# The fourth pair of HGRN2's queries by 512-column products, in a one-core decoder block

## The chip, the cores and the metric

One core of one Trainium2 chip runs the whole kernel as one launch. The metric is the device time of that launch in microseconds (us). TensorE is PE in the profile, its weight loads PEld, VectorE is DVE, ScalarE is ACT, GpSimd is POOL; SP issues most transfers.

## The reference

A decoder block on 256 tokens of width 1024. One input projection feeds two mixers: HGRN2 (8 heads of 128, a gated linear recurrence) and MoBA attention (8 heads of 128; with one block of 256 it is causal attention). Their outputs are projected, gated, merged and projected again; then a layer norm, a SwiGLU feed-forward of 2816, and a second layer norm. Cut to the part that matters here:

```python
proj = einsum('bsd,dn->bsn', x, w_in)
hq, hf, hi, hg, mq, mk, mv, gate_logits = split(proj)
# HGRN2, per head: query, key, value, forget gate
log_f = logaddexp(log(lb), log1p(-lb) + log_sigmoid(hf))
k = (1 - lb) * sigmoid(-hf);  q = silu(hq);  v = hi
scores = einsum('bhtsd,bhtd,bhsd->bhts', decay, q, k)      # decay from the cumulated log_f
o = scores @ v + (q * exp(G)) @ state
y_a = rms_norm(o) * silu(hg)
```

All of it is float32.

## The kernel before

**Products in two parts.** A float32 number is kept as a rounded part and a rest. A weight tile is loaded by SP (`raw`), rounded by ScalarE (`wh`, line 206), and VectorE subtracts to get the rest (`wl`, line 208). x^T is kept in the same way: the `Pair` object `xp` holds both parts next to each other. A product of weights and x is the sum of three: `wh` with the rounded x, `wh` with the rest of x, `wl` with the rounded x. Four tiles of `wh` and four of `wl` are in flight, so a cast into a tile waits for the products that read that tile four loads earlier.

**Two forms for features on the partitions.** `feat_pair` (lines 305 to 307) takes two heads' features at once and issues, per head and per 128 rows of the contraction, three products of 256 columns into one PSUM tile that holds both heads. `wide_pair` (lines 295 and 296) issues one product of 512 columns, `wh` with both parts of x side by side, and one of 256, `wl` with the rounded part; each head has a PSUM tile of its own, whose two halves have still to be added. `add_parts` does that: ScalarE copies one half to `Qg` (line 355) and VectorE adds the other (line 356).

```python
    for j in range(4):
        if j < HQ_WIDE:
            for f, ps in enumerate(wide_pair(f"hq{j}", xp, mm, "mm")):
                z = Qg[:, :, 2 * j + f, :]
                add_parts(z, ps)
                nc.scalar.activation(sgs[f], z, AF.Sigmoid)
        else:
            ps = feat_pair(f"hq{j}")
            nc.scalar.activation(sg, ps, AF.Sigmoid)
```

The queries are four such pairs. Whichever form is used, VectorE then multiplies query, `1 - lb` and sigmoid (line 422) into `Qg`.

**What follows on TensorE.** After the queries come the values, `hi`, in two chunks of 512 columns, then the output gate, `hg`, in two more. `tok_chunk` (lines 341 to 343) makes them: two PSUM tiles per chunk, one for each 128 tokens, 48 products of 512 columns. ScalarE empties `hi` into `hv` (line 583). All these tiles, and those of the queries, come from the pool `mm`, which has four PSUM banks that are handed out in turn. So the first tile of `hg` takes the bank of the first tile of `hi`, and its first product cannot start before ScalarE's first copy to `hv` has ended.

**The recurrence beside it.** `hgrn_steps` runs on VectorE and ScalarE while TensorE makes these projections: `Qt` is `Qg` times the forget gate (line 445), `kq` is key times query (line 460), `pr` the product for the first level (line 481). `kq` and `pr` are folded from 128 to 64 partitions and split in two parts: ScalarE copies one half to `hs` (line 454), VectorE adds the other half (line 455), ScalarE rounds the sum into `kqp` (line 456), VectorE subtracts (line 457). TensorE sums `kqp` over partitions with products `sd` (line 467). Lines 511 and 512 bring `Qt` and `Kt` to the next of seven levels.

**What sets the order.** Parts of the kernel are ordered by hand (`manual_schedule`). The queries, `hi`, `hg`, and all up to the second chunk of the branch merge are not: there a scheduler interleaves the instructions of TensorE, VectorE and ScalarE by its own cost model, and the order that it writes is fixed in the program. Each engine then works through its list in that order and waits on semaphores.

Of the kernel before, what the change touches and what calls it, by code (L numbers as in the profile page):

```python
# [34 lines left out]
EARLY = 4  # L35
HOLD_IN = 2
BLOCKS = 32
HQ_WIDE = 3
HOLD_DOWN = 3
ORDERED = 2  # L40
DOWN = "SSPSSPSSPPP"
# [81 lines left out]
def hybrid_layer_kernel(ctx: ExitStack, tc, x, xw, vecs, bias, wts, ln1_w, ln1_b, ln2_w, ln2_b, consts, out):  # L123
# [162 lines left out]
    def wide_pair(name, a, p, tag):  # L286


        wh, wl = fetch()
        pss = []  # L290
        for f in range(2):
            ps = p.tile([P, 2, T], F32, tag=tag, name=f"{name}{f}")
            wcol = slice(f * P, (f + 1) * P)
            for k in range(KC):
                nc.tensor.matmul(ps, wh[:, k, wcol], a.both(k), start=(k == 0), stop=False)  # L295
                nc.tensor.matmul(ps[:, 0, :], wl[:, k, wcol], a[0, k, slice(0, T)],  # L296
                                 start=False, stop=(k == KC - 1))
            pss.append(ps)
        return pss
# [107 lines left out]
    for j in range(4):  # L407
        sg = sm.tile([P, 2, T], F32, tag="sg", name=f"sgq{j}")
        sgs = [by_half(sg[:, f, :]) for f in range(2)]
        if j < HQ_WIDE:  # L410
            for f, ps in enumerate(wide_pair(f"hq{j}", xp, mm, "mm")):
# [641 lines left out]
```

## Time and profile before

| | |
|---|---|
| Median of 3 runs | 494.98 us (494.71 to 495.24) |
| Profiled execution | 495.12 us, of which the profile's span is 493.3 us |
| Mean granted TensorE clock | 0.998 of full speed |
| Busy: PE, PEld | 485.1 us, 419.5 us |
| Busy: DVE, ACT, POOL | 402.8 us, 287.6 us, 34.7 us |
| Moved by transfers | 92.64 MB, mean 188 GB/s |

In the timelines below a row gives the start and the duration of one instruction in us, its engine, line, operation, the tile written and the tiles read, and, in brackets, how long the engine had been idle before it and for whom. Instructions of one engine overlap by a little, so the time that one takes from its queue is best read from one start to the next.

### The profile page before, as it was taken

What the parts mean: (1) busy time and instruction counts of PE and PEld (TensorE: products, weight loads), DVE (VectorE), ACT (ScalarE), POOL (GpSimd) and SP (SyncE); (2) the same over time, 40 slices, a digit from 0 to 9 for tenths busy, and PEclk for the clock granted to TensorE, in tenths of its full rate; (3) what the DMA queues carried; (4) which work ended last, traced back from release to release, by engine and by line L of the source; (5) the groups of instructions that cost most, each with busy time, mean ns of one, the idle gap of its engine ahead of it and who ended that gap; (6) DMA issues with size and microseconds to landing.
All of it is one profiled execution on the core that took longest, in us unless ns stands there. A gap on an engine that the chain in (4) does not pass through costs nothing.

```text
span 493.3 us, 6696 instructions
## 1 busy us (share of the span) xinstructions
PE 485.1 (98%) x2622; PEld 419.5 (85%) x2622; DVE 402.8 (82%) x513; ACT 287.6 (58%) x390; POOL 34.7 (7%) x33
## 2 busy tenths in 40 slices
PE   9999999999999999999999999999999999999994
PEld 9889888888899888888888888888888888888883
DVE  4889799999767998988765678854887778889996
ACT  6797487444756767777653462444566555475620
POOL 0000000000004441240000000000000000000001
PEclk9999999999999999999999999999999999999999
DMA  8977427534542446348544446255555544365502
GB/s 301 419 275 280 171 90 293 191 151 170 171 170 87 140 169 243 114 171 326 184 159 170 166 179 242 86 188 238 176 192 215 185 170 172 118 230 209 213 0 85
DMA packets 14702, 92.64 MB, mean 188 GB/s; under 512 B 1744, under 2 KB 1744, under 8 KB 4944
## 3 DMA queue, kind: packets, MB, share of 16 engines
q1 hardware_dynamic: 13824, 89.08, 49.2%
q0 software_dynamic: 848, 3.15, 1.8%
q8 instruction: 20, 0.33, 0.3%
q14 instruction: 10, 0.08, 0.0%
HBM read 91.17 MB, written 1.05 MB: 187 GB/s over the span
## 4 chain that ended last, share of the span: by engine, by line
PE 98%; DVE 1%; DVEq 0%; issue 0%
PE fu L295 7%; PE fg L295 7%; PE fg L296 3%; PE fu L296 3%; PE hq L295 2%; PE mk L295 2%; PE mq L295 2%; PE sc L494 2%; PE wp L954 2%; PE wp L956 2%; PE wp L955 2%; PE wp L759 2%; PE wp L758 2%; PE wp L757 2%; PE ga L342 1%; PE ga L343 1%
## 5 line engine op out<-in xcount | busy, mean ns | idle before, releaser
L208 DVE TENSOR_TENSOR wl<-raw,wh 128x2048 fp32r<-128x2048 f32 (+1 forms) x72 | 164.3, 2288 | 51.1 <-ACT wh L206 50.8
L206 ACT CAST wh<-raw 128x2048 fp32r<-128x2048 f32 (+1 forms) x72 | 135.5, 1889 | 60.9 <-PE fg L295 11.5
L295 PE MATMUL fg<-x1p,wh 128*128 128x512 f32 x144 | 50.5, 394 | 0.0
L295 PE MATMUL fu<-x1p,wh 128*128 128x512 f32 x144 | 50.4, 394 | 0.0
L296 PE MATMUL fg<-x1p,wl 128*128 128x256 f32 x144 | 40.0, 278 | 0.0
L296 PE MATMUL fu<-x1p,wl 128*128 128x256 f32 x144 | 39.9, 277 | 0.0
L295 PEld LDWEIGHTS fu<-x1p,wh 128*128 128x128 f32 x144 | 27.0, 187 | 6.2
L295 PEld LDWEIGHTS fg<-x1p,wh 128*128 128x128 f32 x144 | 27.0, 187 | 6.1
L296 PEld LDWEIGHTS fg<-x1p,wl 128*128 128x128 f32 x144 | 27.1, 188 | 0.1
L296 PEld LDWEIGHTS fu<-x1p,wl 128*128 128x128 f32 x144 | 27.1, 188 | 0.0
L295 PE MATMUL mk<-xp,wh 128*128 128x512 f32 x48 | 17.2, 397 | 0.0
L295 PE MATMUL mq<-xp,wh 128*128 128x512 f32 x48 | 17.2, 395 | 0.0
L295 PE MATMUL hq<-xp,wh 128*128 128x512 f32 x48 | 17.0, 399 | 0.0
L758 PE MATMUL wp<-wl,ap 128*128 128x512 f32 (+1 forms) x40 | 14.9, 373 | 0.0
L759 PE MATMUL wp<-wh,ap 128*128 128x512 f32 (+1 forms) x40 | 14.9, 373 | 0.0
L757 PE MATMUL wp<-wh,ap 128*128 128x512 f32 (+1 forms) x40 | 14.9, 373 | 0.0
L541 POOL TENSOR_TENSOR ost<-ost,half 128x4 f32<-128x4 f32 x4 | 4.1, 1013 | 153.1 <-DVE ost L540 153.1
L486 ACT COPY kl<-Kt 128x1024 f32<-128x1024 f32 x6 | 6.5, 1084 | 12.5 <-PE sc L494 7.9
L296 PE MATMUL mk<-xp,wl 128*128 128x256 f32 x48 | 13.7, 285 | 0.0
L296 PE MATMUL mq<-xp,wl 128*128 128x256 f32 x48 | 13.6, 283 | 0.0
L296 PE MATMUL hq<-xp,wl 128*128 128x256 f32 x48 | 13.5, 281 | 0.0
L343 PE MATMUL ga<-wl,xp 128*128 128x512 f32 x32 | 12.7, 398 | 0.0
(346 smaller groups left out, 1343.1 us busy)
## 6 DMA issues: line engine op xcount, KB each, us to landing
raw<-in_wts_dram SPq DMA_DIRECT2D x76, 1024.0 KB, 4.8
xw<-in_xw_dram SPq DMA_DIRECT2D x6, 640.0 KB, 9.0
raw<-in_wts_dram SPq DMA_DIRECT2D x2, 512.0 KB, 11.8
xr<-in_x_dram POOLq DMA_DIRECT2D x1, 1024.0 KB, 5.6
wb<-in_ln_w_dram POOLq DMA_DIRECT2D x2, 512.0 KB, 4.5
wb<-in_ln_b_dram POOLq DMA_DIRECT2D x2, 512.0 KB, 6.9
cst<-in_consts_dram SPq DMA_DIRECT2D x1, 960.0 KB, 13.2
xw<-in_xw_dram SPq DMA_DIRECT2D x2, 384.0 KB, 4.2
```

The lines of the kernel that those rows point to most:

```text
L206: nc.scalar.copy(h[:, ks, :], raw[:, ks, :])
L208: eng.tensor_sub(l[:, ks, :], raw[:, ks, :], r32(h[:, ks, :]))
L295: nc.tensor.matmul(ps, wh[:, k, wcol], a.both(k), start=(k == 0), stop=False)
L296: nc.tensor.matmul(ps[:, 0, :], wl[:, k, wcol], a[0, k, slice(0, T)], start=False, stop=(k == KC - 1))
L343: nc.tensor.matmul(pss[t], ah[:, kk, ts], wl[:, k, :], start=False, stop=(kk == KC - 1))
L494: nc.tensor.matmul(ps[:, a, :], KL[:, h, :], later(Qt, n, h, 1), start=True, stop=True)
L757: nc.tensor.matmul(ps, lh(kk)[:, ts], wh[:, k, ns], start=(kk == first), stop=False)
L758: nc.tensor.matmul(ps, lh(kk)[:, ts], wl[:, k, ns], start=False, stop=False)
L759: nc.tensor.matmul(ps, ll(kk)[:, ts], wh[:, k, ns], start=False, stop=(kk == ktot - 1))
L954: nc.tensor.matmul(ps, ah[:, a, :], wh[:, b, :], start=(q == begins[id(ps)]), stop=False)
L955: nc.tensor.matmul(ps, ah[:, a, :], wl[:, b, :], start=False, stop=False)
L956: nc.tensor.matmul(ps, al[:, a, :], wh[:, b, :], start=False, stop=stop)
```

## The change

One number sets how many of the four pairs of queries use `wide_pair`:

```diff
-HQ_WIDE = 3
+HQ_WIDE = 4
```

The fourth pair (`j` = 3, heads 6 and 7) now has 16 products of 512 columns and 16 of 256 in place of 48 of 256, and takes two banks of `mm` where it took one. One sigmoid of 512 elements on ScalarE becomes two of 256, with two copies (line 355) before them; VectorE has two more additions (line 356), and its two multiplications of line 422 read `Qg` where they read PSUM.

The scheduler orders everything behind it anew. ScalarE, where the fold of `kq` meets the casts of weights and the emptying of `hi` (tile numbers differ by 10 between the two builds; `wh_651` and `wh_641`, `wh_685` and `wh_675` are the same weights, the first two tiles for `hg`), before:

```order
L206 CAST wh_651<-raw_650 128x2048
L454 COPY hs<-kq 64x2048
L206 CAST wh_685<-raw_684 128x2048
L454 COPY hs<-pr 64x1024
L206 CAST wh_715<-raw_714 128x2048
L456 CAST kqp<-hs 64x2048
L583 COPY hv<-hi_0_618 128x512
L583 COPY hv<-hi_1_619 128x512
```

ScalarE at the same place, after:

```order
L206 CAST wh_641<-raw_640 128x2048
L206 CAST wh_675<-raw_674 128x2048
L454 COPY hs<-kq 64x2048
L454 COPY hs<-pr 64x1024
L206 CAST wh_705<-raw_704 128x2048
L456 CAST kqp<-hs 64x2048
L583 COPY hv<-hi_0_608 128x512
L583 COPY hv<-hi_1_609 128x512
```

The second cast of weights for `hg` now stands ahead of the first copy of the fold; `kqp` still stands ahead of the copies to `hv`. VectorE over the same stretch, before:

```order
L445 TENSOR_TENSOR Qt<-Qg,Fg 128x2048
L460 TENSOR_TENSOR kq<-Kt,Qg 128x2048
L208 TENSOR_TENSOR wl_652<-raw_650,wh_651 128x2048
L481 TENSOR_TENSOR pr<-Qt,Kt 128x1024
L455 TENSOR_TENSOR hs<-kq,hs 64x2048
L511 TENSOR_TENSOR Qt<-Qt,Fg 128x512x2
L512 TENSOR_TENSOR Kt<-Kt,Fg 128x512x2
L208 TENSOR_TENSOR wl_686<-raw_684,wh_685 128x2048
L455 TENSOR_TENSOR hs<-pr,hs 64x1024
```

VectorE, after:

```order
L445 TENSOR_TENSOR Qt<-Qg,Fg 128x2048
L460 TENSOR_TENSOR kq<-Kt,Qg 128x2048
L481 TENSOR_TENSOR pr<-Qt,Kt 128x1024
L208 TENSOR_TENSOR wl_642<-raw_640,wh_641 128x2048
L511 TENSOR_TENSOR Qt<-Qt,Fg 128x512x2
L512 TENSOR_TENSOR Kt<-Kt,Fg 128x512x2
L208 TENSOR_TENSOR wl_676<-raw_674,wh_675 128x2048
L455 TENSOR_TENSOR hs<-kq,hs 64x2048
L455 TENSOR_TENSOR hs<-pr,hs 64x1024
```

The sum `hs<-kq` (line 455) moved behind the two level steps of lines 511 and 512 and behind the subtraction for the second `hg` tile. TensorE at the four products `sd`, before (they are the 42nd to 45th of the stretch that begins with `hg`):

```order
L341 MATMUL hg_1_747<-wh_685,xp_83 128x512
L342 MATMUL hg_1_747<-wh_685,xp_83 128x512
L467 MATMUL sd_778<-kqp,ones 128x512
L467 MATMUL sd_781<-kqp,ones 128x512
L467 MATMUL sd_784<-kqp,ones 128x512
L467 MATMUL sd_787<-kqp,ones 128x512
```

TensorE, after (the 33rd to 36th):

```order
L342 MATMUL hg_1_737<-wh_641,xp_82 128x512
L343 MATMUL hg_1_737<-wl_642,xp_82 128x512
L467 MATMUL sd_768<-kqp,ones 128x512
L467 MATMUL sd_771<-kqp,ones 128x512
L467 MATMUL sd_774<-kqp,ones 128x512
L467 MATMUL sd_777<-kqp,ones 128x512
```

They stand nine products earlier. Further on, the products of the levels (`sc`), of the recurrence's output (`o`, `ot`) and of the attention heads stand some products later or earlier among the projections, up to the gate `ga`; behind it the order is the old one. The order of SP's transfers is the same.

## The prediction

> **What bounds the kernel now.** I read the page first, its busy times and its chain of work that ended last.
>
> ```profile
> PE 485.1 (98%) x2622; PEld 419.5 (85%) x2622; DVE 402.8 (82%) x513; ACT 287.6 (58%) x390; POOL 34.7 (7%) x33
> PE 98%; DVE 1%; DVEq 0%; issue 0%
> ```
>
> TensorE is busy for 98% of the span and 98% of the chain is its own. A busy PE can hide waits, since its ends are modelled, so the waits of PE come next. There is a single row, at the start:
>
> ```profile
> PE warm L381 <- PEq L1040: 0.8, 1, 0.8
> ```
>
> So nothing on VectorE or ScalarE costs time today, and nothing there can be gained. Two things can change the time: what TensorE's own products take, and a wait that TensorE does not have now. The timeline of PE, around the queries and behind them, gives the first:
>
> ```profile
> 27.82 0.40 PE L295 MATMUL hq<-xp,wh 128*128 128x512 f32 x1
> ...
> 44.78 0.28 PE L305 MATMUL hq<-xp,wh 128*128 128x256 f32 x1
> ...
> 50.54 0.40 PE L341 MATMUL hi<-wh,xp 128*128 128x512 f32 x1
> ...
> 72.32 0.39 PE L341 MATMUL hg<-wh,xp 128*128 128x512 f32 x1
> ...
> 81.62 1.10 PE L467 MATMUL sd<-kqp,ones 128*128 128x512 f32 x4
> ```
>
> These are the first products of the three wide pairs, of the narrow pair, of `hi`, of `hg`, and `sd`.
>
> **The products themselves.** Three wide pairs take 44.78 - 27.82 = 16.96 us, 5.65 each. The narrow pair takes 50.54 - 44.78 = 5.76. The columns are the same, 768 per head and step, so the change is worth 0.11 us. Its bounds: nothing, if the wide form has no advantage behind another wide pair, and 0.31 us, if a wide pair ran at the rate of `hi` (96 products of 512 columns in 72.32 - 50.54 = 21.78, 0.227 each: 16 x (0.227 + 0.113) = 5.45). I take 0.11, from the rows of the same form. From here on TensorE is 0.11 early: `hi` starts at 50.43, and `hg` is reached at 72.21.
>
> **What the fourth pair adds beside it.** VectorE and ScalarE over this stretch:
>
> ```profile
> 49.01 0.42 DVE L356 TENSOR_TENSOR Qg<-hq,Qg 128x256 f32<-128x256 f32 x1
> ...
> 52.56 2.29 DVE L208 TENSOR_TENSOR wl<-raw,wh 128x2048 fp32r<-128x2048 f32 x1 [2.74 <-ACT wh L206]
> 54.77 0.87 DVE L422 SCALAR_TENSOR_TENSOR Qg<-hq,lb,sgq 128x256 f32<-128x256 f32 x2
> 55.55 0.48 DVE L422 SCALAR_TENSOR_TENSOR Qg<-Qg,lb,sgq 128x256 f32<-128x256 f32 x1
> 56.07 2.29 DVE L445 TENSOR_TENSOR Qt<-Qg,Fg 128x2048 f32<-128x2048 f32 x1
> 58.28 2.28 DVE L460 TENSOR_TENSOR kq<-Kt,Qg 128x2048 f32<-128x2048 f32 x1
> 60.48 2.28 DVE L208 TENSOR_TENSOR wl<-raw,wh 128x2048 fp32r<-128x2048 f32 x1
> 62.68 1.54 DVE L481 TENSOR_TENSOR pr<-Qt,Kt 128x1024 f32<-128x1024 f32 x1
> 64.11 2.28 DVE L455 TENSOR_TENSOR hs<-kq,hs 64x2048 f32<-64x2048 f32 x1
> 66.30 2.24 DVE L511 TENSOR_TENSOR Qt<-Qt,Fg 128x1024 f32<-128x1024 f32 x1
> 68.38 2.27 DVE L512 TENSOR_TENSOR Kt<-Kt,Fg 128x1024 f32<-128x1024 f32 x1
> 70.50 2.27 DVE L208 TENSOR_TENSOR wl<-raw,wh 128x2048 fp32r<-128x2048 f32 x1
> 72.80 1.22 DVE L455 TENSOR_TENSOR hs<-pr,hs 64x1024 f32<-64x1024 f32 x1
> ...
> 76.38 2.29 DVE L457 TENSOR_TENSOR kqp<-hs,kqp 64x2048 fp32r<-64x2048 f32 x1
> ```
>
> ```profile
> 46.67 0.36 ACT L355 COPY Qg<-hq 128x256 f32<-128x256 f32 x1
> ...
> 50.62 1.91 ACT L206 CAST wh<-raw 128x2048 fp32r<-128x2048 f32 x1 [3.26 <-PE hq L306]
> ...
> 55.98 1.92 ACT L206 CAST wh<-raw 128x2048 fp32r<-128x2048 f32 x1 [2.65 <-PE hi L342]
> 60.59 1.91 ACT L454 COPY hs<-kq 64x2048 f32<-64x2048 f32 x1 [2.70 <-DVE kq L460]
> 62.52 1.92 ACT L206 CAST wh<-raw 128x2048 fp32r<-128x2048 f32 x1
> ...
> 66.90 1.92 ACT L206 CAST wh<-raw 128x2048 fp32r<-128x2048 f32 x1 [1.38 <-issue]
> 68.72 1.91 ACT L456 CAST kqp<-hs 64x2048 fp32r<-64x2048 f32 x1
> 70.53 1.54 ACT L583 COPY hv<-hi 128x512 f32<-128x512 f32 x3
> ...
> 74.16 0.57 ACT L583 COPY hv<-hi 128x512 f32<-128x512 f32 x1
> ```
>
> ScalarE gets two copies of 0.36 and one more sigmoid; its idle 3.26 and 2.65 us before the casts at 50.62 and 55.98 hide them. VectorE gets two additions of 0.42. The first falls into its idle 2.74 us before 52.56. The second stands behind the subtraction that ends at 54.7, ahead of the three multiplications (0.39 from start to start, from 54.77 to 55.55 for two): `Qt` begins near 56.25 in place of 56.07, 0.18 late. Alone this costs nothing, since TensorE needs none of it before 81.62. The second PSUM bank costs nothing either: the banks that `hi` takes next are those of the third pair, whose last addition is the row at 49.01, over before `hi` begins.
>
> **The new order, where the cost is.** TensorE cannot start `hg` before ScalarE's first copy to `hv` has ended (its bank). In the trace that copy begins at 70.53 and lasts 0.57, the duration of the single one at 74.16, so it ends at 71.10, 1.2 us ahead of 72.32. On ScalarE's list the cast `kqp` stands right before the copies to `hv`, before and after; `kqp` waits for VectorE's sum `hs<-kq`. In the trace the sum ended at 64.11 + 2.28 = 66.39 and `kqp` had only ScalarE's own queue to wait for. In the new order two level steps and a subtraction stand ahead of the sum. Replayed from start to start:
>
> - `Qt` at 56.25; `kq` 2.21 later (58.28 - 56.07), 58.46; `pr` 2.20 later (60.48 - 58.28), 60.66; the subtraction `wl` 1.43 later (64.11 - 62.68), 62.09.
> - line 511 at 64.29 (+2.20, 62.68 - 60.48); line 512 at 66.37 (+2.08, 68.38 - 66.30); second `wl` at 68.49 (+2.12, 70.50 - 68.38); the sum at 70.69 (+2.20), ended 72.97 (+2.28).
>
> Does anything else hold VectorE there? The second `wl` needs its cast. That cast waits for the last product of `hi` on the old tile: the casts at 55.98 and 66.90 followed the products of their tiles; in the new list of TensorE it is the 48th of `hi`, 50.43 + 48 x 0.227 = 61.33. Cast until 63.2: in time for 68.49. ScalarE's copies of `kq` and `pr` then follow from 63.2 on and end near 66.2, in time for 70.69.
>
> ScalarE: `kqp` starts at 73.00 (a copy follows its VectorE input by 0.03: 60.59 against 58.28 + 2.28), the first copy to `hv` 1.81 later (70.53 - 68.72), 74.81, ended at 75.38. TensorE starts `hg` at about 75.43 in place of 72.21: a wait of 3.2 us. For the release of TensorE by ScalarE I add 0.05; no row shows it alone, and between 0 and 0.1 changes nothing.
>
> What is queued behind the waiting `kqp` on ScalarE: three copies to `hv` and the cast of the fourth `hg` tile, which TensorE reads after 72 more products, some 16 us on. Behind the wait TensorE has no slack anywhere (one PE row in the list of waits), so the 3.2 us go to the end whole.
>
> **Next behind it.** `sd` stands nine products earlier, 32 products after the start of `hg`. It needs line 457's `kqp`; in the trace that ended 78.67 - 72.80 = 5.87 after the start of the `pr` sum, with the same three instructions in between, so now at 72.89 + 5.87 = 78.8. TensorE is there at 75.43 + 32 x 0.227 = 82.7: covered by 3.9 us, and by 0.7 even without the wait. The other moved products (`sc`, `o`, `ot`, heads) I cost at nothing: they sat between projections without one wait in the trace, and have moved by up to a few us with the chain that feeds them. They cannot gain; at worst one of them waits for the length of one more VectorE subtraction, up to 2.3 us. SP's and POOL's queues are passed by nothing that matters.
>
> **Sum.** -0.11 + 3.22 = +3.1 us. On the profiled execution's 495.12 that is 498.2, on the median of the runs, 0.14 lower, 498.1. Its own bounds: lines 511 and 512 took 2.24 and 2.27 for 1024 elements, where the `pr` sum of 1024 elements took 1.22; if they ran at that, the wait shrinks by about 1.8 to 1.4, 496.3. If each of the six steps behind `kq` took the longest spacing seen, 2.30 (72.80 - 70.50), it grows by 0.7 to 3.9, 498.8.
>
> **Rivals.** *The wait does not come (not slower).* Only the fold decides: the copy to `hv` must end by 72.21, so the sum must end by 69.8, 3.2 earlier than worked out. For it: the sum itself needs nothing of the three instructions put ahead of it, and before there was 1.2 us to spare. Against it: an engine works through its list, and VectorE shows no idle row between 56.07 and 76.38 to draw on; three quarters of the two level steps would have to vanish. Then only the products are left: 494.98 - 0.11 = 494.9, or 494.7 at their bound. This is also the case in which the change does just what it says. 0.09.
>
> *The clock falls in the gap.* The rows at the start and the end bear on it:
>
> ```profile
> 0.78 3.65 PE warm L381 x16
> ...
> 5.94 0.41 PE L317 MATMUL hf<-xp,fh 128*128 128x256 f32 x1
> 6.15 0.34 PE L316 MATMUL hf<-xp,fh 128*128 128x256 f32 x1
> ...
> 485.63 0.28 PE L759 MATMUL more<-wh,ap 128*128 128x256 f32 x1
> ```
>
> ```profile
> 484.50:489.00 4.50, 1.41 (x12) 1.21 (x11) 4.25 (x11) 0.00 (x0) 0.92 (x1) 1.00 0.30 117
> 489.00:493.30 4.30, 0.00 (x0) 0.00 (x0) 0.94 (x2) 0.00 (x0) 0.00 (x0) 0.73 0.33 122
> ```
>
> Until 6.15 products of 256 columns come every 0.21 us, against 0.12 in the narrow pair: TensorE started slow and needed 5.4 us of work from 0.78. At the end the granted clock (third number from the right) is 1.00 until 489 and 0.73 on average afterwards; if the low level is half, it lasted 0.27 / 0.5 x 4.3 = 2.3 us, from 491.0 on, 5.1 us after the last product's end near 485.9. A gap of 3.2 us is shorter than that. If it did fall, 5.4 us at 0.12 / 0.21 of the rate lose 2.3 us: 500.4. The Trainium skill ("TensorE: Matmul & The Clock Gate", Part 1) says that the clock halves after an idle window of about 3.4 us, in windows that run freely, and is restored after as long a busy one. By that rule a gap of 3.2 us falls just short of a full window, and one at my upper bound, 3.9, could fill it; its busy window would make the loss an estimated 1.7 us. The trace's 5.1 us at the end agrees with a free-running window. 0.10.
>
> *One of the other moved products waits as well*, up to 2.3 us: 498.4 to 500.4. For it: dozens moved. Against it: no PE wait in the list before, with the same kinds of neighbours. 0.06. *Faster by over 0.2%* would need 1 us from TensorE's own products, three times their bound: 0.02.
>
> **How the numbers follow.** The wait as worked out has 0.73, own range 496.3 to 498.8, and sets the time: 498.1. With the clock case and the second wait above it, 496.3 to 500.5 holds 0.85 or a little more. A measurement of this kernel can tell about 0.2%, 1.0 us, from no change. Slower by more than that: 0.73 + 0.10 + 0.06 = 0.89, of which I give 0.01 to a wait that shrinks below 1 us; within it 0.10; faster 0.02.
>
> **What would show it.** In the changed kernel's list of PE's waits a second row, `hg` line 341 for ACT `hv` line 583, near 3.2 us; ScalarE's `kqp` idle before it, put down to DVE `hs` line 455; that sum starting near 70.7, `kqp` at 73.0, `hg` at 75.4; four equal steps of 5.65 us for the pairs of queries; `sd` near 82.7 without a wait. I am wrong if `hg` starts at 72.2, if the gap is followed by products at twice their spacing, or if another line shows up in that list.

## The result

The changed kernel takes 499.98 us in the median of six runs (498.43 to 501.55), the kernel before beside it 495.08 (494.71 to 495.60): a ratio of 1.0095, 95% interval 1.008 to 1.011. It is slower by 4.9 us, where 3.1 was forecast. The first thing to see is that the runs do not lie around one value: two are at 498.4 to 498.6, two at 499.9 to 500.1, two at 501.5. The kernel before spreads over 0.9 us. One run of the series lag32 further down, 611.38 us at a mean granted clock of 0.751, is in a slow state and is left out of every comparison.

The profiled execution is the quickest, 498.43 us with a span of 496.2. Its page:

```profile
PE 485.1 (98%) x2606; PEld 418.1 (84%) x2606; DVE 402.2 (81%) x515; ACT 288.5 (58%) x393; POOL 32.5 (7%) x33
PE 96%; DVE 2%; DMA 1%; issue 1%; ACT 0%; DVEq 0%
```

TensorE is busy for as long as before, 485.1 us, in a span that is 2.9 us longer, and VectorE's share of the chain has grown from 1% to 2%. The waits of PE name the place:

```profile
PE hg L341 <- ACT hv L583: 3.1, 1, 3.1
PE warm L381 <- PEq L1040: 0.8, 1, 0.8
PE hf L316 <- ACT fh L180: 0.2, 1, 0.2
```

The first row is the one that matters. The last one is new too, but it stands at 4.7 us, ahead of the queries, and two of the kernels below with three wide pairs (sum_late, lag15) have it as well. The chain that ended last, at that place, shows how it comes about (start, duration, what):

```profile
66.91 1.68 DVE Kt L512
68.58 2.12 DVE wl L208
70.70 2.20 DVE hs L455
72.97 1.75 issue
74.73 0.58 ACT hv L583
75.36 0.50 PE hg L341
```

VectorE's level step, subtraction and sum stand on the path one behind the other, as in the order forecast. Their rows in VectorE's timeline, cut to three:

```profile
64.26 2.21 DVE L511 TENSOR_TENSOR Qt<-Qt,Fg 128x1024 f32<-128x1024 f32 x1
66.30 2.28 DVE L512 TENSOR_TENSOR Kt<-Kt,Fg 128x1024 f32<-128x1024 f32 x1
...
70.62 2.27 DVE L455 TENSOR_TENSOR hs<-kq,hs 64x2048 f32<-64x2048 f32 x1
```

The 1.75 us called issue is the time in which ScalarE casts `kqp`, as its timeline shows:

```profile
72.92 1.90 ACT L456 CAST kqp<-hs 64x2048 fp32r<-64x2048 f32 x1 [4.29 <-DVE hs L455]
74.73 1.54 ACT L583 COPY hv<-hi 128x512 f32<-128x512 f32 x3
```

And TensorE, at the first products of the wide pairs and of `hi`, around the wait, and at `sd`:

```profile
27.74 0.40 PE L295 MATMUL hq<-xp,wh 128*128 128x512 f32 x1
...
50.37 0.40 PE L341 MATMUL hi<-wh,xp 128*128 128x512 f32 x1
...
71.91 0.39 PE L343 MATMUL hi<-wl,xp 128*128 128x512 f32 x1
75.36 0.50 PE L341 MATMUL hg<-wh,xp 128*128 128x512 f32 x1 [3.06 <-ACT hv L583]
75.69 0.39 PE L342 MATMUL hg<-wh,xp 128*128 128x512 f32 x1
...
82.75 1.10 PE L467 MATMUL sd<-kqp,ones 128*128 128x512 f32 x4
```

`hg` would have followed the last `hi` product 0.23 us later, at 72.14; it starts at 75.36, 3.22 late. This execution is explained: 495.1 - 0.1 + 3.2 = 498.2, measured 498.43. It does not explain a median of 500. Three theories are set against each other below. A: the wait is all. B: the wait also lowers TensorE's clock in part of the runs. C: something else in the new order, or the wide pair itself, costs the rest.

### The profile page after: what moved, and what is told of

It is laid out like the page before. It is cut to its first block, busy times and chain, and to the rows that moved or that the text cites. A ratio compares the mean times of both kernels' runs of the same rounds, so it can differ in the third digit from the quotient of the medians.

```text
span 496.2 us, 6667 instructions
## 1 busy us (share of the span) xinstructions
PE 485.1 (98%) x2606; PEld 418.1 (84%) x2606; DVE 402.2 (81%) x515; ACT 288.5 (58%) x393; POOL 32.5 (7%) x33
## 4 chain that ended last, share of the span: by engine, by line
PE 96%; DVE 2%; DMA 1%; issue 1%; ACT 0%; DVEq 0%
PE fu L295 7%; PE fg L295 7%; PE fg L296 3%; PE fu L296 3%; PE hq L295 3%; PE mk L295 2%; PE mq L295 2%; PE sc L494 2%; PE wp L955 2%; PE wp L956 2%; PE wp L954 2%; PE wp L758 2%; PE wp L759 2%; PE wp L757 2%; PE hq L296 2%; PE hg L341 2%
## 5 line engine op out<-in xcount | busy, mean ns | idle before, releaser
L295 PE MATMUL hq<-xp,wh 128*128 128x512 f32 x64 | 22.7, 399 | 0.0
L296 PE MATMUL hq<-xp,wl 128*128 128x256 f32 x64 | 18.0, 281 | 0.0
L341 PE MATMUL hg<-wh,xp 128*128 128x512 f32 x32 | 12.6, 393 | 3.1 <-ACT hv L583 3.1
L295 PEld LDWEIGHTS hq<-xp,wh 128*128 128x128 f32 x64 | 12.0, 188 | 3.0
```

The costliest lines, as they stand in the source:

```text
L341: nc.tensor.matmul(pss[t], ah[:, kk, ts], wh[:, k, :], start=(kk == 0), stop=False)
```

## The experiments

Each edit shown is cut to the lines that matter.

**The same kernel again** (no edit).

> The changed kernel once more, for more runs with their span and granted clock. Its six runs so far lie between 498.43 and 501.55 us, at mean clocks of 0.988 to 0.998. Theory A (the wait alone: the first hg product stands 3.1 us for a bank of hi): the spread is chance of single runs, the median comes down to 498.4. Theory B (the wait, and in a part of the runs a granted clock that falls because TensorE stood idle for 3.1 us): runs in two groups again, about 498.4 us at a clock of 0.997 to 0.998 and 499.9 to 501.6 us at 0.988 to 0.994, median between 498.5 and 500.5. Theory C (something else in the new order, a transfer or a later wait, costs 1.5 to 3 us in some runs): the same times, but the clock does not go with them.

Five runs: 499.56, 499.93, 500.00, 500.09 and 501.91 us; ratio 1.0104 (1.0088 to 1.012). None of the five lies near 498.4, where one of the two expected groups was. The profiled execution is the longest of them. The wait row is the same, `PE hg` for `ACT hv`, 3.1 us. The two executions in three stretches (the third number from the right is the granted clock), first the one of 498.43 us, then the one of 501.91:

```profile
72.00:75.20 3.20, 0.29 (x2) 0.00 (x0) 3.14 (x3) 2.28 (x2) 0.00 (x0) 1.00 0.79 307
75.20:82.00 6.80, 6.64 (x29) 5.52 (x30) 5.84 (x3) 4.44 (x6) 0.00 (x0) 1.00 0.40 154
82.00:90.00 8.00, 8.00 (x37) 6.60 (x36) 6.80 (x7) 7.20 (x6) 0.00 (x0) 1.00 0.37 132
```

```profile
72.00:75.20 3.20, 0.85 (x4) 0.38 (x2) 3.14 (x3) 1.73 (x1) 0.00 (x0) 1.00 0.81 297
75.20:82.00 6.80, 6.09 (x14) 4.78 (x15) 6.40 (x3) 5.00 (x7) 0.00 (x0) 0.50 0.46 169
82.00:90.00 8.00, 8.00 (x36) 6.56 (x35) 3.40 (x5) 3.83 (x3) 0.00 (x0) 1.00 0.36 131
```

Behind the same wait the clock is at 1.00 in the one and at 0.50 for 6.8 us in the other, with 14 products in place of 29. The timeline of the second gives the spacing:

```profile
75.91 0.79 PE L341 MATMUL hg<-wh,xp 128*128 128x512 f32 x1 [3.06 <-ACT hv L583]
76.50 0.63 PE L342 MATMUL hg<-wh,xp 128*128 128x512 f32 x1
76.92 0.63 PE L343 MATMUL hg<-wl,xp 128*128 128x512 f32 x1
...
82.04 0.39 PE L343 MATMUL hg<-wl,xp 128*128 128x512 f32 x1
82.27 0.40 PE L341 MATMUL hg<-wh,xp 128*128 128x512 f32 x1
```

0.43 us from product to product, then 0.23 from 82.04 on. Products ran at half clock from 75.9 to 82.0: half of 6.1 us is 3.1 lost, and 498.43 + 3.1 = 501.5 of 501.91. The six runs of both series near 500 have mean clocks of 0.992 to 0.995, where the two short ones have 0.997 and 0.998. Of the three longest, two have 0.988 and 0.989; the third, 501.45 us, has 0.994, as if half as much had been lost, and its last 1.5 us stay unexplained. The mean over a whole run is a rough sign: it varies from 0.995 to 0.998 in the kernel before. A is out; B has its profile.

**The sum ahead again, with the wide pair kept.**

```diff
-        fold(kqp, kq, slice(0, 2048), up, down)
+        total = fold(kqp, kq, slice(0, 2048), up, down)   # fold returns its tensor_add
...
-            nc.vector.tensor_mul(flat(later(Qt, n)), flat(later(Qt, n)), first)
-            nc.vector.tensor_mul(flat(earlier(Kt, n)), flat(earlier(Kt, n)), second)
+            with tc.issue_after(total.ins):
+                nc.vector.tensor_mul(flat(later(Qt, n)), flat(later(Qt, n)), first)
+                nc.vector.tensor_mul(flat(earlier(Kt, n)), flat(earlier(Kt, n)), second)
```

> The changed kernel with its wide fourth pair, but VectorE's sum of the fold (L455) kept ahead of L511 and L512, as before the change. The sum then starts near 66.7 instead of 70.6 us, kqp near 69.0, and the first hv copy near 70.9, ahead of the end of the hi products at 72.2. Theories A and B: no wait of hg, 494.9 us (494.5 to 495.4), clock 0.998, all runs close together; the wide pair is worth its -0.1 us and nothing else. Theory C (the cost lies in the wide pair or in the rest of its new order): 496.5 to 498 us, with runs spread over 1.5 us or more.

495.06 us in eleven runs (494.94 to 495.61), ratio 0.9998 (0.9989 to 1.0007). VectorE and ScalarE in its timeline:

```profile
67.00 2.29 DVE L455 TENSOR_TENSOR hs<-kq,hs 64x2048 f32<-64x2048 f32 x1
```

```profile
69.33 1.92 ACT L456 CAST kqp<-hs 64x2048 fp32r<-64x2048 f32 x1 [0.16 <-DVE hs L455]
71.15 1.53 ACT L585 COPY hv<-hi 128x512 f32<-128x512 f32 x3
```

The sum stands ahead of the level steps again, though still behind both subtractions. The first copy to `hv` is over before the last `hi` product (72.45), and the wait is gone, together with the spread. So the wide pair alone is worth its tenth of a microsecond or nothing, and that half of C is out. The scheduler also orders other products anew behind the `hg` products in this build, so that this run alone does not rule out the rest of the order; the experiments that follow do. This is the best version that the runs point to, and it equals the kernel before.

**The wait kept, TensorE busy in it.**

```diff
+            if q == 1 and name == "hi1":
+                idle = aux.tile([P, 512], F32, tag="aux", name="idle")
+                for i in range(13):     # end: the last hi product
+                    with tc.issue_after(end.ins):
+                        end = nc.tensor.matmul(idle, xTh[:, 0, 0:P], xp.both(0), start=True, stop=True)
```

> The changed kernel, with 13 more products of 512 columns between the last hi product and the first hg product, into a bank that nobody reads: the wait of 3.1 us stays, but TensorE works through about 13 x 0.227 = 2.95 us of it. Theory A: 498.4 us. Theory B: also 498.4 us (498.1 to 498.9), but every run at a clock of 0.997 to 0.998 and none at 499.9 or above. Theory C: runs between 498.4 and 501.5 us as in the changed kernel.

498.48 us in five runs (498.28 to 498.84), ratio 1.0069 (1.0056 to 1.0081). TensorE in its timeline:

```profile
72.25 0.39 PE L345 MATMUL hi<-wl,xp 128*128 128x512 f32 x1
72.48 3.11 PE L350 MATMUL idle<-xp 128*128 128x512 f32 x13
75.70 0.50 PE L343 MATMUL hg<-wh,xp 128*128 128x512 f32 x1
```

`hg` starts 3.22 us late, as in the changed kernel, and no run reaches 499. Thirteen products that nobody reads make the kernel 1.5 us faster in the median. What the changed kernel loses beyond its wait is the idle time's effect on the clock, not the delay of any work.

**The sum moved in the kernel before.** Three wide pairs; the products of `pr` and of the first level are written inside the fold, ahead of its sum:

```diff
             nc.scalar.copy(s, src[b, :])
-            nc.vector.tensor_add(s, src[a, :], s)
+            ins = behind()          # pr, then lines 511 and 512 of level 0
+            with tc.issue_after(ins.ins) if ins else ExitStack():
+                nc.vector.tensor_add(s, src[a, :], s)
```

> The kernel before (three wide pairs), with VectorE's sum hs<-kq put behind the two level steps L511 and L512, but ahead of the subtraction wl. The sum then starts near 64.1 + 4.3 = 68.4 us, kqp near 70.7, the first hv copy near 72.5, hg near 73.1 instead of 72.3. Theory A and B: PE waits 0.8 us for hv (0.6 to 1.1), 496.0 us (495.7 to 496.4), the clock steady, since the wait is shorter than lag15's. Theory C (the place of the sum is not what makes hg wait, or only beside the wide pair): 495.15 us.

496.15 us in ten runs (496.01 to 496.74), ratio 1.0023 (1.0014 to 1.0032). The waits and the timelines of VectorE, ScalarE and PE:

```profile
PE hg L341 <- ACT hv L595: 0.7, 1, 0.7
```

```profile
68.40 2.28 DVE L457 TENSOR_TENSOR hs<-kq,hs 64x2048 f32<-64x2048 f32 x1
```

```profile
70.72 1.92 ACT L458 CAST kqp<-hs 64x2048 fp32r<-64x2048 f32 x1 [1.92 <-DVE hs L457]
72.53 1.54 ACT L595 COPY hv<-hi 128x512 f32<-128x512 f32 x3
```

```profile
73.16 0.50 PE L341 MATMUL hg<-wh,xp 128*128 128x512 f32 x1 [0.69 <-ACT hv L595]
```

Every start is within 0.1 us of the one expected. Two of the three instructions that the changed kernel puts ahead of the sum make 0.85 us of late start by themselves, without the fourth wide pair; the subtraction is the third.

**Idle times of several lengths in the kernel before.** GpSimd adds over the first part of `hv`, one small product waits for the last add, and the first `hg` product stands behind it. The `for` line gives the sizes of the adds, in columns, for each run.

```diff
+    for n in [512, 256]:            # lag15 [512], lag20 [384, 128], lag32 [512, 384], lag38 [512, 512], lag3 3 x [512]
+        nc.gpsimd.tensor_add(late[:, 0:n], src[:, 0:n], src[:, 0:n])
+        src = late
+    with tc.issue_after(held[-1].ins):          # the last hi product
+        held.append(nc.tensor.matmul(idle[:, 0:64], late[:, 0:P], late[:, P:P + 64], start=True, stop=True))
```

> The kernel before (three wide pairs), with a wait of about the same length put at the same place: GpSimd adds three times over 128x512 after the first hv copy (1.3 us each by its adds in the trace), one small product waits for the last, and the first hg product stands behind that. The gap should be about 3.0 us (2.8 to 3.4). Theory A: 495.1 + 3.0 = 498.1 us, runs close together. Theory B: 498.1 us in some runs and 499.5 to 501.5 us at a lower clock in others. Theory C (the wide pair or its order spreads the runs): 498.1 us, runs within 0.5 us and the clock at 0.998.

> The kernel before with a wait made at the same place, shorter than the changed kernel's: one add of GpSimd over 128x512 after the first hv copy (2.47 us beside VectorE, as lag3 showed), a small product that waits for it, then the hg products. TensorE idle for about 1.4 us, the first hg product about 1.7 us late. Theory A (the wait alone): 495.15 + 1.7 = 496.9 us. Theory B (a long enough idle time also halves the granted clock for some us): too short for that, 496.9 us (496.5 to 497.3), clock at 0.995 to 0.998, runs close together.

> As lag15, with GpSimd's first add over 128x384 and a second over 128x128: TensorE idle for about 2.0 us, between lag15 (1.2 us, no run with a lower clock) and lag26 (2.8 us, five of six). Theory A: 497.6 us. Theory B: 497.6 us (497.2 to 498.0) at a steady clock if 2.0 us is still too short, or some runs at 499 to 501 us at a clock of 0.988 to 0.995 if the bound lies below 2 us.

> As lag15, with a second add over 128x256: TensorE idle for about 2.6 us, the first hg product about 3.0 us late. Theory A: 498.1 us. Theory B: 498.1 us if 2.6 us is still too short; else part of the runs at 499.5 to 501.5 us with a clock of 0.988 to 0.995.

> As lag15, with a second add over 128x384: TensorE idle for about 3.2 us, as in the changed kernel, the first hg product about 3.5 us late; no wide fourth pair and none of its order. Theory A: 498.6 us, clock steady. Theory B: most runs 1 to 3.5 us above that, at 499.6 to 502.1 us, with the clock lower the longer the run, and a few near 498.7.

> As lag15, with a second add over 128x512: TensorE idle for about 3.8 us, the first hg product about 4.1 us late. Theory A: 499.3 us, clock steady. Theory B: every run with the clock at half for some us behind the idle time, 1 to 3.5 us more: 500.3 to 502.8 us.

Their rows in the lists of PE's waits, in the order lag15, lag20, lag26, lag32, lag38, lag3, one fence each:

```profile
PE idle L600 <- POOL late L596: 1.2, 1, 1.2
```

```profile
PE idle L600 <- POOL late L596: 2.4, 1, 2.4
```

```profile
PE idle L600 <- POOL late L596: 2.8, 1, 2.8
```

```profile
PE idle L600 <- POOL late L596: 3.0, 1, 3.0
```

```profile
PE idle L600 <- POOL late L596: 3.2, 1, 3.2
```

```profile
PE idle L600 <- POOL late L596: 6.2, 1, 6.2
```

The table sets each run against the wait alone. "Late" is the start of the first `hg` product in the profile, less that of the last `hi` product and 0.23; "base" is the kernel before (495.15, for lag20 and sum_late 495.03) plus late, and for the changed kernel and fill13 less 0.1 for the wide pair. In lag38 and lag3 the small product itself already ran at half clock, so that some 0.2 us of the clock's loss is counted in "late".

| kernel | PE idle | late | base | runs less base |
|---|---|---|---|---|
| sum_late | 0.7 | 0.85 | 495.9 | 0.1 to 0.9, ten runs |
| lag15 | 1.2 | 1.64 | 496.8 | -0.2 to 0.5, five runs |
| lag20 | 2.4 | 2.77 | 497.8 | 0.2, 0.2, 0.3, 0.7; 1.8, 2.0 |
| lag26 | 2.8 | 3.18 | 498.3 | -0.1; 1.5, 1.6, 1.6, 1.7; 3.3 |
| lag32 | 3.0 | 3.39 | 498.5 | 0.4; 1.5, 1.6; 3.3 |
| changed, 11 runs | 3.1 | 3.22 | 498.3 | 0.1, 0.3; 1.3, 1.6, 1.6, 1.7, 1.8, 1.8; 3.2, 3.3, 3.6 |
| lag38 | 3.2 | 3.81 | 499.0 | 1.4, 1.6, 2.2, 2.8 |
| lag3 | 6.2 | 6.85 | 502.0 | 1.8, 2.1, 2.5, 3.1 |
| fill13 | none | 3.22 | 498.3 | 0.0 to 0.5, five runs |

Up to 1.2 us of idle time nothing is added. From 2.4 us on a part of the runs pays more, at 2.8 to 3.1 us most of them, at 3.2 and 6.2 all; lag26 and lag32 give the changed kernel's times without its wide pair and its order, so C is out. The granted clock of lag26's profiled run (1.6 above base), then of lag3's:

```profile
75.90:79.10 3.20, 3.20 (x10) 2.42 (x9) 3.17 (x2) 0.00 (x0) 0.00 (x0) 0.50 0.47 148
```

```profile
76.00:82.60 6.60, 4.07 (x11) 3.30 (x12) 6.54 (x3) 0.00 (x0) 2.48 (x1) 0.50 0.54 201
```

In lag26 the clock falls at 75.90, half a microsecond after `hg` has begun (75.44), and comes back at 79.31: 3.41 us, of which half, 1.7, is lost. In lag3 it falls inside the idle time, at 76.00, and comes back at 82.83; products use the last 4.3 us of that (from 78.53), and 2.1 are lost. Stretches of 3.41 and 6.83 us thus make the two sizes of the table, 1.6 and 3.3, and those between where a part of the stretch is idle.

When the clock falls, and for how long, can be read from the times at which the granted clock changes. Within each of the twelve profiled executions these times lie whole multiples of 3.413 us apart: in `again` 6.93, 75.19, 82.02 and 495.03, with distances of 20, 2 and 121 times that. So each trace can be cut into windows of 3.413 us, from its own changes, and TensorE's idle time be counted in each (by its rows, whose ends are modelled). Around the gap:

| execution | window, us | idle in it, us | clock in it | clock behind it |
|---|---|---|---|---|
| changed, 498.43 us | 70.44 to 73.85 | 1.56 | full | full |
| | 73.85 to 77.27 | 1.50 | full | full |
| again, 501.91 us | 71.78 to 75.19 | 2.35 | full | half |
| | 75.19 to 78.61 | 0.71 | half | half |
| | 78.61 to 82.02 | 0 | half | full |
| lag26, 499.97 us | 72.49 to 75.90 | 2.71 | full | half |
| | 75.90 to 79.31 | 0 | half | full |
| lag32, 498.89 us | 70.76 to 74.17 | 1.41 | full | full |
| | 74.17 to 77.58 | 1.57 | full | full |

The same idle time of 3.06 us is split 1.56 and 1.50 by a window's end in the one execution of the changed kernel, and lies with 2.35 us in one window in the other. Over all windows of the twelve executions, those at the end of the program included, the clock fell behind each window at full clock with 2.35 us or more idle, and behind none with 1.81 us or less. It came back behind windows with at most 0.31 us idle, and not behind those with 0.68 and 0.71 (both in `again`): the idle time that reaches into the window behind the fall makes the second stretch.

The Trainium skill ("TensorE: Matmul & The Clock Gate", Part 1) gives freely running windows of 3.4 us after which the clock is set anew. The two lengths agree with one and two of them, and so does the chance from run to run. Its other half, that a whole idle window is needed, does not agree: 2.35 us of idle time in a window was enough in `again`. The bound in these runs lies between 1.81 and 2.35 us of a window.

Three idle times of this series came out other than expected. lag3 was to leave 3.0 us idle and left 6.2, since its three adds ran from 70.98 to 78.48, 7.5 us and not 3.9; lag38 left 3.2 us for 3.8, lag20 2.4 for 2.0.

## Why the prediction was right, and where it was short

- *The products*: 5.66 us for each of four pairs ((50.37 - 27.74) / 4) against 5.65 forecast; `hi` starts at 50.37 against 50.43, since the first pair began 0.08 earlier (27.74 against 27.82). sum_first shows the size in the time: -0.1 us, not distinguishable from nothing.
- *The chain of the wait*: the sum at 70.62 (70.69 forecast), `kqp` at 72.92 (73.00), `hv` at 74.73 (74.81), `hg` at 75.36 (75.43). Each lies 0.07 or 0.08 early, as the first pair does: the replay from start to start held for all six steps, and the lower bound, level steps at 1.2 us, was never near (2.21 and 2.28). sum_late confirmed the terms one by one.
- *What is behind it*: `sd` at 82.75 (82.7), without a wait. No row behind `hg` appears among PE's waits in either execution, so the third rival is out there; the first, that the wait does not come, is out too.
- *The step that failed* is the chance of the clock's fall, 0.10. "A gap of 3.2 us is shorter than that" took the 5.1 us from the last product to the fall at the end of the program for a length that a gap must have. Cut into windows, that trace shows 1.63 us left of a window that had been busy enough, then one whole idle window (487.54 to 490.96); in `again` the same distance is only 2.40 us (492.63 to 495.03). A gap of 3.06 us needs to lie with some 2 us in one window, not to be as long as one; the runs put the fall at nine in eleven. It was the likeliest case, and the forecast should have been 495.0 + 3.1 + some 1.6 = 499.7, against 499.98 measured. One of the prediction's own signs of being wrong, products at twice their spacing behind the gap, is there in `again`.
- *Its price* was also put too simply: one loss of 2.3 us, from the start of the program. It is 1.6 or 3.3 us, by one or two stretches at half clock. The range to 500.5 held the median only because this rival and a second wait had been counted into it, and this rival's price happens to lie between the two sizes; the wait as worked out, 496.3 to 498.8, held two of eleven runs, and three lie above 500.5.
- *A bound*: six steps at 2.30 us in place of the 12.23 worked out would add 1.6 us to the wait, not 0.7; 0.7 comes out when the step of 1.43 is left as it is. Nothing measured hangs on it.

## What to carry to other kernels

Where TensorE is the bound, ask of every change what it does to the lists of the engines that empty its banks: here one sum, put three instructions later on VectorE, cost 3.2 us, and the change that caused the new order gave 0.1. Price a new idle time of TensorE twice, by its length and, once some 2 us of it can lie in one window of 3.41, by a stretch at half clock behind it; run it often enough to see whether the times fall into groups. If such a wait cannot be removed, products that nobody reads can be worth their place in it.

## What was not expected of the hardware

GpSimd's adds and multiplications over 128x512 (lines 647 and 648) take 1.3 to 1.5 us in 14 of 16 cases in the kernel before, and 2.19 and 3.12 in the other two. In lag3 the first add took 2.47 us and the other two 4.95 together, and VectorE slowed beside them. GpSimd, then VectorE, in lag3:

```profile
70.98 2.47 POOL L596 TENSOR_TENSOR late<-hv 128x512 f32<-128x512 f32 x1 [70.54 <-ACT hv L591]
73.53 4.95 POOL L596 TENSOR_TENSOR late<-late 128x512 f32<-128x512 f32 x2
```

```profile
70.28 2.27 DVE L211 TENSOR_TENSOR wl<-raw,wh 128x2048 fp32r<-128x2048 f32 x1
72.58 1.95 DVE L463 TENSOR_TENSOR hs<-pr,hs 64x1024 f32<-64x1024 f32 x1
74.56 3.02 DVE L211 TENSOR_TENSOR wl<-raw,wh 128x2048 fp32r<-128x2048 f32 x1
77.61 3.01 DVE L465 TENSOR_TENSOR kqp<-hs,kqp 64x2048 fp32r<-64x2048 f32 x1
80.65 2.29 DVE L211 TENSOR_TENSOR wl<-raw,wh 128x2048 fp32r<-128x2048 f32 x1
```

The subtraction that takes 2.29 us alone (80.65) takes 3.02 while GpSimd adds (until 78.48), and the sum of `pr` 1.95 where it took 1.22 in the kernel before; the subtraction at 70.28, whose last microsecond and a half also lay beside an add, took its usual 2.27. The second row of GpSimd holds two adds; the first of the two ends near 75.43.

The ends of the rows fit two engines that take turns, one whole instruction each. The three adds end at 73.45, 75.43 and 78.48, each 0.90 us after the end of the VectorE instruction that had begun before it (72.55, 74.53, 77.58). The three slowed VectorE instructions end 1.08, 2.15 and 2.14 us after the adds, about what each takes undisturbed. That is a reading of one trace: which of the operands the two engines contend for was not tried.
